# Context products in plain fp32 from the unsplit weights, and ten dot products moved to another place of the order

## The chip, the cores and the metric

One Trainium2 chip, one core of it. The metric is the device time of one execution in microseconds (us), the median of several runs. An execution runs five engines side by side, each with a queue of its own that it works through in order: TensorE (PE, its weight loads PEld), VectorE (DVE), ScalarE (ACT), GpSimd (POOL, idle here) and SyncE (SP), which issues all transfers.

## What is computed

A diffusion backbone of two layers over 1024 latent tokens and 256 context tokens of width 1024. Layer 0 mixes by a gated linear recurrence in both directions, layer 1 by a short convolution, and each is followed by a gated feed-forward part. Shift, scale and gate of each sub-layer come from a product of the conditioning vector with a large matrix. What the change touches is this part of layer 0:

```python
hl = modulate(rms_norm(x, norm_mix_g[l]), sm, cm)
hc = modulate(rms_norm(h_ctx, norm_mix_g[l]), smc, cmc)
ul = seq_conv(hl @ w_x, conv_w, conv_b, CONV_A_PAD)
uc = seq_conv(hc @ w_x, conv_w, conv_b, CONV_A_PAD)
hl_f, hc_f = rglru_direction(ul, uc, w_r[0], b_r[0], w_i[0], b_i[0], lam[0], False)
hl_b, hc_b = rglru_direction(ul, uc, w_r[1], b_r[1], w_i[1], b_i[1], lam[1], True)
yl = (jax.nn.gelu(hl @ w_gate) * (hl_f + hl_b).astype(hl.dtype)) @ w_out
```

The context only gives the recurrence its starting state. `adaln` is `jax.nn.silu(cvec) @ w + b`, split into six vectors.

## The kernel before

Data lies with channels on the 128 partitions, so a vector of width 1024 is eight chunks. To keep fp32 accuracy at the full rate of TensorE, each operand is split into two fp32r halves: the high half is a copy that ScalarE makes (`wh`, `bh`, `uh`), the low half the rest, which VectorE makes by a subtraction (`wl`, `bl`, `ul`). `mm` (L432 and after) issues three matmuls for one product: high by high, high by low, low by high.

The program is written as a list of units, each a function with the weights that it needs as keys. `run_units` (L369) walks the list. Before each unit it issues as many loads as it finds a free raw tile for, and prepares as many weights ahead as it finds free slots for. There are three raw tiles (`raw0`, shown as raw_95, raw_96 and raw_97 in the rows of the order) of 128x1024 in this part of the kernel, and room for three split weights. A raw tile counts as free as soon as the preparation of its weight is written down, since the split empties it.

The calls aren't issued at once: `Plan.record` (L66, its emission L165, which is why all instructions have that one line) collects them, and `Plan.flush` (L121) puts them in order by its own costs and due times, at `open_mx`, at `open_ffn` and at the end. TensorE's instructions keep the order of the units.

`ORDER` (L45) lists the units of layer 0's mixer. `g2` to `g7` are the gate products. `ctx` normalises the context (`ctx_apply`) into hch and hcl, and makes eight units `wx_ctx` (L744), one per chunk m, called xc0 to xc7 here: eight steps of three matmuls of 256 columns, then a convolution by one pass on ScalarE and three on VectorE (`conv_a`). `mx` closes the context's pool (`cs6`, the normalised context, `xc`, `ccb`), flushes, and opens in the same memory the tile `mx`, seven slots of 128x1280, in which the recurrence works. `x4` to `x7` are the latent products with `w_x`, each with a convolution. `us0` splits chunks 0 and 1 of the latent and context u into uh and ul (`u_split`, L727) for the recurrence blocks `r0` and `r1`, and so on in pairs. A block `r0` to `r7` (`ri`, L778) makes the products with two weights (called ri0 and ri1 for r0 and r1), writes them through tanh into slots of mx on ScalarE, and runs the elementwise chain and the two scans on VectorE with exp and sqrt on ScalarE between.

`e6` and `d3`, `d2`, `d1` are the modulation dots (`ahead_dots`, L864): each loads 512 KB of the matrix and reduces it with the conditioning vector in one pass on VectorE. `e` puts the data into slots of mx in turn, `d` into the one tile `acct`. Six stand in `e6`, thirteen in the `d` between the blocks.

Of the kernel before, what the change touches and what calls it, by code (L numbers as in the profile page):

```python
# [8 lines left out]
F32 = mybir.dt.float32  # L9
F32R = mybir.dt.float32r  # L10
AF = mybir.ActivationFunctionType
ALU = mybir.AluOpType

P = 128
D = 1024
KD = 8
SEQ = 1024
HALF = 512
CTX = 256
# [11 lines left out]
for _n, _w in _VEC:  # L31
# [10 lines left out]
DOTS = (0, 0, 0, 1, 1, 2, 2, 2)  # L42


ORDER = ("g2 shift g3 norm g4 g5 ctx mx us0 e6 x4 r0 d3 x5 d2 r1 d2 us2 x6 d1 r2 d1 x7 d1 r3 d1 us4 d1 r4 d1 g6 r5 "  # L45
         "us6 g7 r6 r7")

TABLE = {AF.Silu: (AF.Silu, AF.Tanh), AF.Gelu_apprx_tanh: (AF.Gelu_apprx_tanh, AF.Tanh), AF.Sqrt: (AF.Sqrt,),
         AF.Exp: (AF.Exp, AF.Tanh), AF.Tanh: (AF.Exp, AF.Tanh)}
# [134 lines left out]
def hybrid_kernel(ctx: ExitStack, tc: tile.TileContext, out, xs, cs, c, cc, ada, vecs,  # L184
                  ident, w0, wx, wg, wo, wri, wbi, wbo, wup, wdn):
    nc = Plan(tc)
    V, S, T, G = nc.vector, nc.scalar, nc.tensor, nc.gpsimd
# [20 lines left out]
    def bank():  # L208
        return ptile[:, ring("bank", 4)]
# [6 lines left out]
    def stt(o, a, s, b, op0=ALU.mult, op1=ALU.add, eng=None):  # L216
        (eng or V).scalar_tensor_tensor(out=o, in0=a, scalar=s, in1=b, op0=op0, op1=op1)
# [10 lines left out]
    def act(o, i, f, bias=0.0, scale=1.0):  # L228
        S.activation(o, i, f, bias=bias, scale=scale)
# [21 lines left out]
    def vcol(name, i):  # L251
        return vec[:, VOFF[name] + i:VOFF[name] + i + 1]

    x = xp.tile([P, KD, SEQ], F32, tag="x", name="x")
# [25 lines left out]
    wslots = [(wh0, wl0, i) for i in range(6)]  # L280

    def unit(fn, *keys):
        units.append((fn, keys))
        return len(units) - 1

    class Raw:

        def __init__(self, src, after=-1, pool="raw"):
            self.src, self.after, self.pool, self.left, self.tile = src, after, pool, 0, None

    class Item:

        def __init__(self, key, raws, n, prep, after=-1):
            self.key, self.raws, self.n, self.prep, self.after = key, raws, n, prep, after
            for r in raws:
                r.left += 1

    items = {}

    def wsrc(key):  # L300
        kind = key[0]
        if kind in ("x", "xc"):
            return wx[key[1]]
        if kind == "g":
            return wg[key[1]]
        if kind == "o":
            return wo[key[1]]
        if kind == "ri":
            return wri[key[1]]
        if kind == "bo":  # L310
            return wbo[key[1]]
        return wdn[key[1], key[2], :, 2 * D:]

    def dot(dst, raw, bt, eng=None):

        if eng is G:
            mul(raw, raw, bt, G)
            S.activation(raw, raw, AF.Identity, bias=0.0, scale=1.0, accum_out=dst)
        else:
            V.scalar_tensor_tensor(out=raw, in0=raw, scalar=1.0, in1=bt, op0=ALU.mult, op1=ALU.mult, accum_out=dst)  # L320
# [4 lines left out]
    def weight_item(key):  # L325
        src = wsrc(key)
        n = src.shape[-1]

        def prep(sl, raws):
            hi, lo = flat(sl[0][0], sl[0][2], len(sl))[:, :n], flat(sl[0][1], sl[0][2], len(sl))[:, :n]  # L330
            split(hi, lo, raws[0].tile[:, :n], weight_hi[0])
            return hi, lo
        return Item(key, [Raw(src)], -(-n // HALF), prep)
# [35 lines left out]
    def run_units(nside):  # L369


        stream, seen, last = [], {}, {}
        for i, (_, keys) in enumerate(units):
            for k in keys:
                if k not in seen:
                    seen[k] = i
                    stream.append(items[k] if k in items else weight_item(k))
                    for _ in range(nside(k)):
                        if side:
                            src, dst, bt, eng = side.pop(0)  # L380
                            stream.append(Item(None, [Raw(src)], 0, lambda sl, raws, dst=dst, bt=bt, eng=eng:
                                               dot(dst, raws[0].tile, bt, eng)))
                last[k] = i
        loads = {"raw": [], "s": []}
        for it in stream:
            for r in it.raws:
                if r not in loads[r.pool]:
                    loads[r.pool].append(r)
        free, pos = [True] * 64, 0
        occ, rp = {n: {} for n in loads}, dict.fromkeys(loads, 0)  # L390
        live, np_ = {}, 0
        for i, (fn, keys) in enumerate(units):
            while True:
                moved = False
                for name, todo in loads.items():
                    tiles = raw0 + more.get("raw", []) if name == "raw" else more.get("stage", [])
                    while todo and todo[0].after < i:
                        at = [(rp[name] + j) % len(tiles) for j in range(len(tiles))]
                        at = [j for j in at if j not in occ[name] or not occ[name][j].left]
                        if not at:  # L400
                            break
                        r = todo.pop(0)
                        r.tile = tiles[at[0]]
                        if len(r.src.shape) == 3:
                            nc.sync.dma_start(r.tile.rearrange("p (a b) -> p a b", a=r.src.shape[1]), r.src)
                        else:
                            nc.sync.dma_start(r.tile[:, :r.src.shape[-1]], r.src)
                        occ[name][at[0]] = r
                        rp[name], moved = at[0] + 1, True
                while np_ < len(stream):  # L410
                    it = stream[np_]
                    if it.after >= i or any(r.tile is None for r in it.raws):
                        break
                    n = len(wslots)
                    at = [(pos + j) % n for j in range(n)]
                    at = [j for j in at if j % max(it.n, 1) == 0 and all(free[j:j + it.n])]
                    if not at:
                        break
                    sl = list(range(at[0], at[0] + it.n))
                    if it.n:  # L420
                        pos = (at[0] + it.n) % n
                    for j in sl:
                        free[j] = False
                    for r in it.raws:
                        r.left -= 1
                    live[it.key] = (it.prep([wslots[j] for j in sl], it.raws), sl)
                    np_, moved = np_ + 1, True
                if not moved:
                    break
            fn(*[live[k][0] for k in keys if k[0] != "act"])  # L430
            for k in keys:
                if last[k] == i:  # L432
                    for j in live.pop(k)[1]:
                        free[j] = True

    def mm(ps, w, wi, rh, rl, start, stop, **o):

# [5 lines left out]
    def mmk(ps, w, rhi, rlo, s):  # L443
        n = len(rhi)
        for k in range(n):
            mm(ps[:, s], w, slice(k * P, (k + 1) * P), rhi[k][:, s], rlo[k][:, s], k == 0, k == n - 1)
# [100 lines left out]
    cpx = ExitStack()  # L547
    cp = cpx.enter_context(tc.tile_pool(name="cp", bufs=1))
    cs6 = cp.tile([P, 6, CTX], F32, tag="cs6", name="cs6")
    hch = cp.tile([P, KD, CTX], F32R, tag="hch", name="hch")  # L550
    hcl = cp.tile([P, KD, CTX], F32R, tag="hcl", name="hcl")
    xc = cp.tile([P, KD, CTX], F32, tag="xc", name="xc")
    ccb = cp.tile([P, D], F32, tag="ccb", name="ccb")
    uc = up.tile([P, KD, CTX], F32, tag="uc", name="uc")
# [154 lines left out]
    def ctx_apply():  # L709
        make_ab(1, modc, 0, 0, 1, "norm_mix_g")  # L710
        A, B = ab(1)
        for k in range(KD):
            u = cs6[:, 2 + k % 4]
            stt(u, xc[:, k], A[k], rc[0], ALU.mult, ALU.mult)
            act(hch[:, k], u, AF.Identity, bias=B[k])
            stt(hcl[:, k], u, B[k], hch[:, k].bitcast(F32), ALU.add, ALU.subtract)

    def conv_a(z, u, m):

        n = z.shape[-1]  # L720
        w = [vcol("a_conv_w", t * 8 + m) for t in range(4)]
        act(u, z, AF.Identity, bias=vcol("a_conv_b", m), scale=w[2])
        stt(u[:, 1:], z[:, :n - 1], w[1], u[:, 1:])
        stt(u[:, 2:], z[:, :n - 2], w[0], u[:, 2:])
        stt(u[:, :n - 1], z[:, 1:], w[3], u[:, :n - 1])
# [16 lines left out]
        unit(f, ("x", m))  # L742

    def wx_ctx(m):  # L744
        def f(w):
            z = bank()
            mmk(z, w, [hch[:, k] for k in range(KD)], [hcl[:, k] for k in range(KD)], slice(0, CTX))
            conv_a(z[:, :CTX], uc[:, m], m)
        unit(f, ("xc", m))

    def gate(m):
# [119 lines left out]
    shifts = start()  # L871
    for o in ORDER.split():
        if o[0] == "g":
# [510 lines left out]
    def nside(key):  # L1384
        return 4 if key in (("g", 2), ("g", 3)) else 0
# [59 lines left out]
```

## Time and profile before

| | us |
|---|---|
| median of 3 runs | 2079.51 (2079.14 to 2079.75) |
| the profiled execution | 2082.59 |
| its span | 2080.8 |
| TensorE busy | 2036.8 (98%) |
| VectorE busy | 1764.5 (85%) |
| ScalarE busy | 1049.3 (50%) |

All rows come from the one profiled execution, whose span is the time from its first instruction to its last. Starts are counted from the span's start. A group of equal instructions has its count, its busy time and the mean of one; instructions of one engine overlap at their ends, so that starts lie closer together than the durations tell. What stands behind an arrow is what an engine waited for.

### The profile page before, as it was taken

To read this page: it belongs to the slowest core of one execution; us is meant where nothing else is said; L and a number is where in the kernel's file an instruction comes from. 1 tells how busy PE (TensorE), PEld (TensorE's weight loads), DVE (VectorE), ACT (ScalarE), POOL (GpSimd) and SP (SyncE) were. 2 spreads that over 40 slices of the span, in tenths; PEclk is the share of its full clock that TensorE was granted. 3 is DMA by queue.
4 is the path that set the end of the run, shared out by engine and by line. 5 is a ranking of instruction groups with operands and counts; after the bars stand their busy time and mean duration, and the time that the engine had idled before them with its cause. 6 is when DMAs were issued, how large, how long until landed. Compare 5 with 4: busy or idle time off the path is not lost.

```text
span 2080.8 us, 25029 instructions
## 1 busy us (share of the span) xinstructions
PE 2036.8 (98%) x9218; PEld 1681.5 (81%) x9218; DVE 1764.5 (85%) x2624; ACT 1049.3 (50%) x1574; POOL 0.2 (0%) x4
## 2 busy tenths in 40 slices
PE   8899989999999999999999999999999999999998
PEld 6688877787888888878888788888888888878888
DVE  7998999979888888798769988858988887688867
ACT  6366878546544444535255433435644444464345
POOL 0000000000000000000000000000000000000000
PEclk9999999999999999999999999999999999999999
DMA  7544222551334455565361345652243443474345
GB/s 298 185 169 162 71 81 84 193 167 48 126 132 157 156 174 173 174 199 162 95 194 66 114 164 197 231 192 75 83 136 128 142 137 108 137 236 142 111 140 164
DMA packets 103418, 307.05 MB, mean 148 GB/s; under 512 B 10368, under 2 KB 14720, under 8 KB 103168
## 3 DMA queue, kind: packets, MB, share of 16 engines
q1 hardware_dynamic: 103296, 305.46, 44.6%
q8 instruction: 72, 1.18, 0.2%
q14 instruction: 50, 0.41, 0.1%
HBM read 248.80 MB, written 56.62 MB: 147 GB/s over the span
## 4 chain that ended last, share of the span: by engine, by line
PE 84%; DVE 9%; ACT 4%; DMA 2%; issue 1%; SPq 0%; DVEq 0%; ACTq 0%
PE banks L165 84%; ACT mx L165 2%; DVE x L165 2%; DVE mx L165 2%; DVE u L165 2%; DVE bl L165 2%; DMA x<-in_xs 1%; DVE wl L165 1%; DMA s<-bd 1%; ACT L165 1%; ACT bh L165 1%; DMA raw<-in_wg 0%; DVE uc L165 0%; DVE ul L165 0%; DVE acct L165 0%
## 5 line engine op out<-in xcount | busy, mean ns | idle before, releaser
L165 PE MATMUL banks<-bl,wh 128*128 128x512 f32 (+1 forms) x2720 | 1052.2, 387 | 11.0 <-DVE bl L165 10.9
L165 PE MATMUL banks<-bh,wh 128*128 128x512 f32 (+1 forms) x2720 | 1054.3, 388 | 3.2 <-ACT wh L165 1.6
L165 PE MATMUL banks<-bh,wl 128*128 128x512 f32 (+1 forms) x2720 | 1051.0, 386 | 2.6 <-DVE wl L165 2.5
L165 PEld LDWEIGHTS banks<-bl,wh 128*128 128x128 f32 x2720 | 511.6, 188 | 124.7 <-DVE bl L165 21.6
L165 PEld LDWEIGHTS banks<-bh,wh 128*128 128x128 f32 x2720 | 511.8, 188 | 109.0 <-ACT wh L165 2.0
L165 PEld LDWEIGHTS banks<-bh,wl 128*128 128x128 f32 x2720 | 511.6, 188 | 108.1 <-DVE wl L165 7.3
L165 ACT ACTIVATE wh<-raw 128x512 fp32r<-128x512 f32 (+2 forms) x386 | 275.6, 717 | 475.0 <-PE banks L165 394.7
L165 DVE TENSOR_TENSOR wl<-raw,wh 128x512 fp32r<-128x512 f32 (+2 forms) x386 | 303.2, 794 | 60.4 <-ACT wh L165 56.9
L165 DVE SCALAR_TENSOR_TENSOR x<-banks,mod,x 128x512 f32<-128x512 f32 (+1 forms) x184 | 132.6, 726 | 93.3 <-PE banks L165 92.3
L165 ACT ACTIVATE s<-banks 128x512 f32<-128x512 f32 x174 | 103.8, 596 | 195.0 <-PE banks L165 191.8
L165 ACT ACTIVATE wh<-s 128x512 fp32r<-128x512 f32 x216 | 135.5, 628 | 110.4 <-DVE s L165 63.7
L165 DVE TENSOR_TENSOR wl<-s,wh 128x512 fp32r<-128x512 f32 x216 | 148.5, 688 | 38.6 <-ACT wh L165 34.9
L165 DVE TENSOR_TENSOR s<-s,banks 128x512 f32<-128x512 f32 x158 | 107.8, 683 | 37.4 <-PE banks L165 36.9
L165 DVE SCALAR_TENSOR_TENSOR x<-s,vec,x 128x504 f32<-128x504 f32 x132 | 96.4, 740 | 10.2 <-ACT x L165 9.0
L165 DVE SCALAR_TENSOR_TENSOR acct<-acct,cb 128x1024 f32<-128x1024 f32 x69 | 84.1, 1218 | 4.5 <-DMA acct<-in_ada 4.5
L165 PE MATMUL banks<-uh,wh 128*128 128x512 f32 (+1 forms) x192 | 70.8, 369 | 8.1 <-ACT mx L165 7.0
L165 PE MATMUL banks<-ul,wh 128*128 128x512 f32 (+1 forms) x192 | 70.5, 367 | 3.1 <-DVE ul L165 3.1
L165 PE MATMUL banks<-uh,wl 128*128 128x512 f32 (+1 forms) x192 | 70.2, 366 | 0.0
L165 ACT ACTIVATE bh<-s 128x512 fp32r<-128x512 f32 x88 | 51.5, 624 | 35.3 <-DMA s<-bd 34.0
L165 ACT ACTIVATE bh<-x,cols 128x512 fp32r<-128x512 f32 x64 | 45.1, 721 | 42.1 <-DVE cols L165 27.3
L165 DVE TENSOR_TENSOR x<-x,s 128x512 f32<-128x512 f32 x90 | 61.0, 686 | 0.8
L165 DVE TENSOR_TENSOR bl<-s,bh 128x512 fp32r<-128x512 f32 x88 | 57.2, 684 | 5.0 <-ACT bh L165 5.0
(154 smaller groups left out, 1702.0 us busy)
## 6 DMA issues: line engine op xcount, KB each, us to landing
raw<-in_wup SPq DMA_DIRECT2D x92, 512.0 KB, 3.6
acct<-in_ada SPq DMA_DIRECT2D x69, 512.0 KB, 3.5
bd<-x SPq DMA_DIRECT2D x48, 512.0 KB, 3.2
s<-bd SPq DMA_DIRECT2D x44, 512.0 KB, 4.5
raw<-in_wdn SPq DMA_DIRECT2D x32, 512.0 KB, 4.4
raw<-in_wdn SPq DMA_DIRECT2D x40, 384.0 KB, 3.4
raw<-in_wbi SPq DMA_DIRECT2D x26, 512.0 KB, 4.1
u<-in_ada SPq DMA_DIRECT2D x24, 512.0 KB, 4.6
```

Source lines behind the costliest of these rows:

```text
L165: getattr(getattr(self.tc.nc, e), op)(*a, **k)
```

## The change

The products of the context no longer use split operands. `wx_ctx` takes the raw weight tile as it was loaded and the normalised context in one fp32 tile `hc`, and issues one plain fp32 matmul for each of the eight steps. Its item is marked `hold`: the raw tile stays taken until the unit is done. The two context tiles hch and hcl become the one `hc`. In the order, `e6` becomes `e16`, and of the thirteen dots in `d` ten go: three `d1` are left.

```diff
-ORDER = ("g2 shift g3 norm g4 g5 ctx mx us0 e6 x4 r0 d3 x5 d2 r1 d2 us2 x6 d1 r2 d1 x7 d1 r3 d1 us4 d1 r4 d1 g6 r5 "
-         "us6 g7 r6 r7")
+ORDER = "g2 shift g3 norm g4 g5 ctx mx us0 e16 x4 r0 x5 r1 us2 x6 d1 r2 x7 d1 r3 us4 d1 r4 g6 r5 us6 g7 r6 r7"
...
-        def __init__(self, key, raws, n, prep, after=-1):
-            self.key, self.raws, self.n, self.prep, self.after = key, raws, n, prep, after
+
+        def __init__(self, key, raws, n, prep, after=-1, hold=False):
+            self.key, self.raws, self.n, self.prep, self.after, self.hold = key, raws, n, prep, after, hold
             for r in raws:
                 r.left += 1
...
-        if kind in ("x", "xc"):
+        if kind == "x":
             return wx[key[1]]
...
                     for r in it.raws:
-                        r.left -= 1
-                    live[it.key] = (it.prep([wslots[j] for j in sl], it.raws), sl)
+                        r.left -= not it.hold
+                    live[it.key] = (it.prep([wslots[j] for j in sl], it.raws), sl, it.raws if it.hold else [])
                     np_, moved = np_ + 1, True
...
                 if last[k] == i:
-                    for j in live.pop(k)[1]:
+                    _, sl, held = live.pop(k)
+                    for j in sl:
                         free[j] = True
+                    for r in held:
+                        r.left -= 1
...
-    hch = cp.tile([P, KD, CTX], F32R, tag="hch", name="hch")
-    hcl = cp.tile([P, KD, CTX], F32R, tag="hcl", name="hcl")
+    hc = cp.tile([P, KD, CTX], F32, tag="hc", name="hc")
...
             stt(u, xc[:, k], A[k], rc[0], ALU.mult, ALU.mult)
-            act(hch[:, k], u, AF.Identity, bias=B[k])
-            stt(hcl[:, k], u, B[k], hch[:, k].bitcast(F32), ALU.add, ALU.subtract)
+            act(hc[:, k], u, AF.Identity, bias=B[k])
...
     def wx_ctx(m):
+
         def f(w):
             z = bank()
-            mmk(z, w, [hch[:, k] for k in range(KD)], [hcl[:, k] for k in range(KD)], slice(0, CTX))
+            for k in range(KD):
+                T.matmul(z[:, :CTX], w[:, k * P:(k + 1) * P], hc[:, k], start=k == 0, stop=k == KD - 1)
             conv_a(z[:, :CTX], uc[:, m], m)
+        items["xc", m] = Item(("xc", m), [Raw(wx[m])], 0, lambda sl, rs: rs[0].tile, hold=True)
         unit(f, ("xc", m))
```

What this does to the order of the queues stands at three places. First SP's queue from the loads of the last context weights on (in_wx are the weights of xc and x, in_wri those of the blocks, in_ada the rows of the dots). Before:

```order
L165 DMA raw_96<-in_wx 128x1024
L165 DMA raw_97<-in_wx 128x1024
L165 DMA raw_95<-in_wri 128x1024
L165 DMA raw_96<-in_wri 128x1024
L165 DMA raw_97<-in_wx 128x1024
L165 DMA raw_95<-in_wx 128x1024
L165 DMA raw_96<-in_wri 128x1024
L165 DMA mx_1235<-in_ada 128x1024 x6
L165 DMA acct_73<-in_ada 128x1024
```

With the change, from the loads of xc7 (raw_96) and x4 (raw_97) on:

```order
L164 DMA raw_96<-in_wx 128x1024
L164 DMA raw_97<-in_wx 128x1024
L164 DMA raw_95<-in_wx 128x1024
L164 DMA raw_97<-in_wri 128x1024
L164 DMA raw_96<-in_wri 128x1024
L164 DMA raw_97<-in_wri 128x1024
L164 DMA raw_97<-in_wx 128x1024
L164 DMA mx_1082<-in_ada 128x1024 x16
L164 DMA raw_97<-in_wri 128x1024
```

Before, x4, ri0, ri1 and x5 take the three tiles in turn (raw_97, raw_95, raw_96, raw_97). Now all four go into raw_97, each behind the split of the one before it, because raw_95 and raw_96 are held for xc6 and xc7; what frees these two goes to x6 (raw_95) and the first weight of r2 (raw_96). The loads of the dots stand behind them, sixteen in one row instead of six.

VectorE's queue around block r0. Before, from the low half of ri1's split on:

```order
L165 TENSOR_TENSOR wl_94<-raw_96,wh_93 128x1024
L165 SCALAR_TENSOR_TENSOR uc_109<-banks_72,vec_75,uc_109 128x255
L165 SCALAR_TENSOR_TENSOR uc_109<-banks_72,vec_75,uc_109 128x254
L165 SCALAR_TENSOR_TENSOR uc_109<-banks_72,vec_75,uc_109 128x255
L165 TENSOR_TENSOR ul_112<-u_110,uh_111 128x1024 x2
L165 TENSOR_TENSOR ul_112<-uc_109,uh_111 128x256 x2
L165 SCALAR_TENSOR_TENSOR mx_1235,mod_78<-mx_1235,cb_74 128x1024 x2
L165 SCALAR_TENSOR_TENSOR x_85<-banks_72,vec_75,x_85 128x1023
L165 SCALAR_TENSOR_TENSOR x_85<-banks_72,vec_75,x_85 128x1022
L165 SCALAR_TENSOR_TENSOR x_85<-banks_72,vec_75,x_85 128x1023
L165 TENSOR_TENSOR wl_94<-raw_97,wh_93 128x1024
L165 SCALAR_TENSOR_TENSOR mx_1235,mod_78<-mx_1235,cb_74 128x1024 x4
```

With the change, from the splits of ri0 and ri1 on:

```order
L164 TENSOR_TENSOR wl_94<-raw_97,wh_93 128x1024 x2
L164 TENSOR_TENSOR ul_111<-u_109,uh_110 128x1024 x2
L164 SCALAR_TENSOR_TENSOR x_85<-banks_72,vec_75,x_85 128x1023
L164 SCALAR_TENSOR_TENSOR x_85<-banks_72,vec_75,x_85 128x1022
L164 TENSOR_TENSOR ul_111<-uc_108,uh_110 128x256 x2
L164 SCALAR_TENSOR_TENSOR mx_1082,mod_78<-mx_1082,cb_74 128x1024 x2
L164 SCALAR_TENSOR_TENSOR x_85<-banks_72,vec_75,x_85 128x1023
L164 TENSOR_TENSOR wl_94<-raw_97,wh_93 128x1024
L164 SCALAR_TENSOR_TENSOR mx_1082,mod_78<-mx_1082,cb_74 128x1024 x10
L164 SCALAR_TENSOR_TENSOR mx_1082<-mx_1082,u_109 128x1024
L164 SCALAR_TENSOR_TENSOR mx_1082,mod_78<-mx_1082,cb_74 128x1024 x3
L164 SCALAR_TENSOR_TENSOR u_109<-mx_1082,u_109 128x1024
```

The rows with mod_78 are dots, x_85 the convolution of x4, ul the low halves of u for r0 and r1. The splits of ri0 and ri1 now follow each other, ahead of ul; twelve dots instead of six stand ahead of the first elementwise step of r0 (mx<-mx,u), three more ahead of the second.

ScalarE's queue at the same place. Before, from the high half of ri1's split (raw_96) on:

```order
L165 ACTIVATE wh_93<-raw_96 128x1024
L165 ACTIVATE uc_109<-banks_72,vec_75 128x256
L165 ACTIVATE uh_111<-u_110 128x1024 x2
L165 ACTIVATE uh_111<-uc_109 128x256 x2
L165 ACTIVATE x_85<-banks_72,vec_75 128x1024
L165 ACTIVATE wh_93<-raw_97 128x1024
```

With the change, from the split of x4 on:

```order
L164 ACTIVATE wh_93<-raw_97 128x1024
L164 ACTIVATE uc_108<-banks_72,vec_75 128x256
L164 ACTIVATE wh_93<-raw_97 128x1024 x2
L164 ACTIVATE uh_110<-u_109 128x1024 x2
L164 ACTIVATE x_85<-banks_72,vec_75 128x1024
L164 ACTIVATE uh_110<-uc_108 128x256 x2
L164 ACTIVATE wh_93<-raw_97 128x1024
```

The uh copies still stand behind the split of ri1, which now is the third of the splits out of raw_97.

## Rows read from the trace of the kernel before

**Rows 1.** Engine totals: busy us, share of the span, instructions.

```profile
PE 2036.8 (98%) x9218; PEld 1681.5 (81%) x9218; DVE 1764.5 (85%) x2624; ACT 1049.3 (50%) x1574; POOL 0.2 (0%) x4
```

**Rows 2.** Busy time by stage: stretch, length, PE, PEld, DVE, ACT, POOL, clock, DMA, GB/s.

```profile
146.80:169.80 23.00, 23.00 (x193) 23.00 (x192) 20.61 (x32) 12.58 (x16) 0.00 (x0) 1.00 0.49 160
...
205.60:393.30 187.70, 174.75 (x814) 145.11 (x813) 184.05 (x184) 149.87 (x158) 0.00 (x0) 0.96 0.26 86
```

**Rows 3.** Waits of TensorE, 170 to 420 us: total us, times, longest.

```profile
PE banks L165 <- ACT mx L165: 7.0, 2, 4.3
...
PEld banks L165 <- ACT mx L165: 9.0, 4, 4.8
```

**Rows 4.** Timeline (start, us): the first context product, and the matmul behind the last.

```profile
146.79 0.28 PE L165 MATMUL banks<-hch,wh 128*128 128x256 f32 x1
...
169.83 0.40 PE L165 MATMUL banks<-bh,wh 128*128 128x512 f32 x1
```

**Rows 5.** Timeline around a plain fp32 matmul of 256 columns (cs,ones, two records).

```profile
124.36 0.40 PE L165 MATMUL banks<-bh,wl 128*128 128x512 f32 x1
124.36 0.42 PEld L165 LDWEIGHTS banks<-cs,ones 128*128 128x128 f32 x2
124.59 0.59 PE L165 MATMUL banks<-cs,ones 128*128 128x256 f32 x2
...
125.25 0.40 PE L165 MATMUL banks<-bl,wh 128*128 128x512 f32 x1
125.48 0.39 PE L165 MATMUL banks<-bh,wl 128*128 128x512 f32 x1
```

**Rows 6.** Groups, 0 to 420 us: the halves of a weight's split (busy, mean ns).

```profile
L165 DVE TENSOR_TENSOR wl<-raw,wh 128x1024 fp32r<-128x1024 f32 x39 | 47.2, 1218 | 3.2 <-ACT wh L165 3.1
...
L165 ACT ACTIVATE wh<-raw 128x1024 fp32r<-128x1024 f32 x39 | 40.7, 1055 | 32.1 <-PE banks L165 22.6 <-issue 6.2 <-DMA raw<-in_wg 2.0
```

**Rows 7.** Transfers issued from 130 to 240 us, with the median us to landing.

```profile
raw<-in_wx SPq DMA_DIRECT2D x10, 512.0 KB, 4.3
raw<-in_wri SPq DMA_DIRECT2D x6, 512.0 KB, 4.0
mx<-in_ada SPq DMA_DIRECT2D x6, 512.0 KB, 7.2
```

**Rows 8.** Transfers issued from 187 to 230 us, when few others ran.

```profile
raw<-in_wri SPq DMA_DIRECT2D x3, 512.0 KB, 3.4
```

**Rows 9.** Timeline before and at block r0, ScalarE, SP, VectorE, TensorE.

```profile
171.32 2.00 ACT L165 ACTIVATE uh<-u 128x1024 fp32r<-128x1024 f32 x2
...
172.63 3.17 SPq L165 DMA_DIRECT2D mx<-in_ada  x6
...
173.57 2.35 DVE L165 TENSOR_TENSOR ul<-u,uh 128x1024 fp32r<-128x1024 f32 x2
175.84 0.75 DVE L165 TENSOR_TENSOR ul<-uc,uh 128x256 fp32r<-128x256 f32 x2
177.86 1.22 DVE L165 SCALAR_TENSOR_TENSOR mx<-mx,cb 128x1024 f32<-128x1024 f32 x1 [1.27 <-DMA mx<-in_ada]
...
180.74 0.39 PE L165 MATMUL banks<-uh,wh 128*128 128x512 f32 x1
...
187.14 1.22 DVE L165 SCALAR_TENSOR_TENSOR mx<-mx,cb 128x1024 f32<-128x1024 f32 x1
...
188.29 1.22 DVE L165 SCALAR_TENSOR_TENSOR mx<-mx,cb 128x1024 f32<-128x1024 f32 x1
```

**Rows 10.** Groups of VectorE, 169.8 to 393.3 us: the thirteen dots in acct.

```profile
L165 DVE SCALAR_TENSOR_TENSOR acct<-acct,cb 128x1024 f32<-128x1024 f32 x13 | 15.8, 1217 | 0.0
```

**Rows 11.** Busy time from the end of ul on, to and behind the end of r0.

```profile
176.60:223.10 46.50, 45.99 (x225) 38.85 (x225) 38.48 (x41) 32.35 (x34) 0.00 (x0) 1.00 0.31 112
223.10:393.30 170.20, 157.76 (x729) 130.74 (x728) 166.72 (x171) 136.33 (x143) 0.00 (x0) 0.96 0.27 88
```

**Rows 12.** Busy time of one stretch, with the granted clock behind POOL.

```profile
270.00:300.00 30.00, 23.94 (x96) 19.35 (x97) 29.64 (x33) 22.28 (x25) 0.00 (x0) 0.83 0.28 88
```

## The prediction

> **What bounds the kernel now.** I read the engine totals first, then the windows by stage, the waits of TensorE, the order of the queues, and last the timeline around the change. Over the whole span TensorE is busy 98%, VectorE 85% [rows 1], so later stages pass any delay on. The change touches one stretch, in which the bound changes hands [rows 2]. The context products, 146.8 to 169.8 us, keep TensorE busy throughout, VectorE for 20.6 of 23.0 us. From 205.6 to 393.3 us, the recurrence blocks, VectorE is busy 184.05 of 187.7 us and TensorE has 13 us idle; what TensorE waits for there are tanh writes of ScalarE into the mx slots, 7.0 and 9.0 us [rows 3], and these wait for VectorE to free a slot. So a microsecond of VectorE's work is worth most after 205 us, and one of TensorE's inside the context products. The change takes dots from the first place and pays in the second. What decides is when the dots and the weights of the first block can start.
>
> **The change, part by part.**
>
> The products. Before, 192 matmuls of 256 columns run from 146.79 to 169.83 us [rows 4]: 23.04 us, 0.120 each. After there are 64 plain fp32 ones. Their price stands in one place: the fp32 matmul of 256 columns at 124.59, two records, lies between bh,wl at 124.36 and bl,wh at 125.25; those 0.89 us hold it and two ordinary matmuls of 0.227 (125.25 to 125.48), so it costs 0.89 - 0.454 = 0.436 us, with its two weight loads [rows 5]. 64 x 0.436 = 27.9 us: **TensorE +4.9 us**, 3.49 us a product instead of 2.88, ending at 174.7 instead of 169.8. Starts are read to 0.01 us, so it is at least 0.425; if each record took as long as an ordinary 512-column matmul it would be 0.454: +4.2 to +6.0.
>
> Weight loads, against a rule. The fp32 pair's two weight loads take 0.42 us together and lie beside the matmul [rows 5]. The Trainium skill (TensorE: Matmul & The Clock Gate, section Weight-path perf modes) says that the fast weight load is off for FP32 operands, which speaks against this change. By its 128 columns at 1.2 GHz, an estimate of 0.107 us, 128 loads that nothing hid would add 13.7 us. The row shows them hidden, and my sum has nothing for them; the other case is a rival below.
>
> Splits that fall away. Eight context weights are no longer split: 8 x 1.055 us on ScalarE and 8 x 1.22 on VectorE [rows 6] (a little less there, since neighbours overlap at their ends), and eight hcl halves. That is some 12 us of VectorE's time, but it lies before 171 us, where TensorE is the bound; it buys nothing unless something useful takes its place. By the order nothing does: the sixteen dots load into mx, which lies on the context pool's memory, and their loads stand in SP's queue behind the raw loads of x4, ri0, ri1 and x5.
>
> The held tiles. This is the main term. A context weight now keeps its raw tile until its products are done, so xc6 and xc7 hold raw_95 and raw_96, and x4, ri0, ri1 and x5 all pass through raw_97, one load and one split after the other. Loads take 4.3, 4.0 and, alone, 3.4 us from issue to landing [rows 7, 8]. xc5 ends at 146.8 + 6 x 3.49 = 167.7 and frees raw_97 at 167.9. x4: landed 172.2, ScalarE's half 173.3, VectorE's (behind the conv of xc6) 174.6, just in time for TensorE at 174.7. ri0: landed 178.6, split 180.9. ri1: landed 184.3, ScalarE 185.4, VectorE 186.6. ScalarE's uh copies for block r0, 1.0 us each [rows 9], stand behind ri1's split in its queue, VectorE's ul behind its other half: ul 0 and 1 end at 187.7 and 188.8. Before, they ended at 175.9, 5 us ahead of block r0 at 180.7 [rows 9]. After, TensorE is through x4 at 185.6 and reaches the product that needs ul 1 at 186.5: it stalls 2.3 us. VectorE then does two of x4's three conv passes (2.5 us) and the two small ul halves: 192.0. Before it stood there, without those passes, at 176.6 [rows 9]: **VectorE is 15.4 - 2.5 = 12.9 us late.** x5's load goes out at 186.6 and the dots' behind it; the first mx load landed 5.2 us after its issue before (172.6 to 177.8 [rows 7, 9]), so the first dot runs at about 192.2.
>
> A price by a rule. The Trainium skill (DMA: Bandwidth & Descriptors, section Anatomy of one DMA) fits 2.0 us plus the bytes at 436 GB/s, 3.2 us for 512 KB, measured on another issue path; by that estimate the three loads would take 9.6 us, not 11.7, and the time would be 2.1 us lower. No load here landed in under 3.4 us [rows 7, 8], so I keep the rows.
>
> The dots. Nineteen dots follow that point on VectorE in either version, 6 + 13 before [rows 10] and 16 + 3 after, 1.145 us apart where they follow each other (starts at 187.14 and 188.29 [rows 9]). So the ten buy no time after it; moving them only changes what VectorE's idle time hides. Twelve of them now stand ahead of the first elementwise step of r0 instead of six, and they reuse the seven mx slots into which r0's tanh values must go, so ScalarE's tanh waits for dots that wait for loads. At the end of r0 I make VectorE 192.0 + 38.5 (its work from 176.6 to 223.1 [rows 11]) + 9 x 1.145 more dots - 2.5 = 238.3 us without any idle time, against 223.1.
>
> Idle time, the only thing to win back. From 176.6 to 393.3 us VectorE idled 8.0 + 3.5 = 11.5 us before [rows 11], most of it inside r0. After: about 3 us up to the end of r0 (dots waiting for the second round of slots, and the exp to sqrt chain), the same 3.5 later, and 2 us because nine dots that covered waits for ScalarE are gone there (10.3 us of work; I take a fifth as uncovered, bounds none and all). Sum 8.5.
>
> **Sum:** 12.9 - 11.5 + 8.5 = +9.9 us at the end of block r7. TensorE doesn't set that end: it has 170.2 - 157.8 = 12.4 us idle after 223 [rows 11]. Behind it everything is as before with a few splits exchanged, 0 with no cover in it: TensorE is nearly full, and the delay passes on. The profiled execution is 2082.59 us (span 2080.8 and 1.8 around it), so its counterpart would be 2092.5; it lies 3.1 above the median of the runs, 2079.51, and on that I predict **2089.4 us**. With no idle time left it would be 12.9 - 11.5 = +1.4; with all ten us uncovered +18; loads of 3.4 or 4.5 us shift it by 2 either way.
>
> **Rivals.**
> VectorE catches up: the order after r0, freed of dots, closes nearly all gaps. For: 3.5 us idle in 170 were all that was left before, so it is a packed queue; against: it must be packed in r0 too, where loads and slots pace it. +1.4 to +4 us, 2081 to 2083.5.
> The relief wins (the other side): the recurrence is VectorE's, ten dots fewer there are 11.5 us, less the products' 4.9, so -6.6 and 2072.9. It decides if the sixteen dots are done by the end of x4, about 186 us, in VectorE's idle time. For: the 98% busy blocks; against: SP's order, in which their loads come after x5's, by my chain at 187.
> Weight loads of plain fp32 don't hide behind the matmuls: 64 pairs of 0.42 us [rows 5] are 26.9 us more on TensorE, 2116 with the rest. Against: the one pair in the trace hid them.
> A second delay: TensorE's stalls at r0 and r1 let its clock fall, as after the idle stretch from 270 us, when TensorE was busy 23.94 of 30 us and the mean granted clock was 0.83 of full speed, a third of the time at the lower level of 1.2 GHz [rows 12]. That lost 30 x 0.17 = 5.1 us there; on top of the forecast 2094.5.
> That the change doesn't do what its words say is in the forecast: the dots come after the products, not beside them.
>
> **How the numbers follow.** A measurement of this kernel can tell about 0.2% (4.2 us) from no change. Forecast 0.62, with +4.5 to +16; second delay 0.12; unhidden loads 0.04: slower 0.78. VectorE catches up 0.15: same. Relief wins 0.07: faster. The range leaves out the relief, the unhidden loads and part of the catching up: 2081.0 to 2097.0.
>
> **What would show it.** Right: 64 fp32 products at 0.43 to 0.45 us, 27 to 29 us together; in the waits, TensorE or ScalarE waiting for uh, ul or wh at about 185 to 189 us; the four loads into raw_97 one behind the other's split; the first mx load issued near 187; VectorE largely idle from 147 to 190, and r0 ended near 240 us; r7's end near 403. Wrong: mx loads issued before 180, r0 ended before 232, products over 0.5 us each, or VectorE with well over 10 us idle after 240.

## The result, and the profile after

The changed kernel took **2092.12 us** (median of 6 runs, 2091.31 to 2093.06), the kernel before beside it 2079.63 (2079.04 to 2081.68): a ratio of 1.0059, 95% interval 1.0046 to 1.0072, **12.5 us slower**. The profiled execution took 2093.05 us, its span 2091.3.

The group of the context products, TensorE from 140 to 180 us (busy us, mean ns), is the counterpart of the 192 matmuls of [rows 4]:

```profile
L164 PE MATMUL banks<-hc,raw 128*128 128x256 f32 x128 | 27.8, 379 | 0.0
```

128 records are 64 matmuls: 0.434 us each, 27.8 us in place of 23.2. Busy time by stage, cut at the start of these products, 2.7 us behind their end, at the end of the split of u, at the end of r0 and of r7 (columns as in [rows 2]):

```profile
144.20:174.80 30.60, 30.60 (x142) 26.76 (x142) 12.71 (x25) 6.48 (x10) 0.00 (x0) 1.00 0.42 139
174.80:189.20 14.40, 12.69 (x47) 9.54 (x46) 7.84 (x9) 6.78 (x8) 0.00 (x0) 0.89 0.49 177
189.20:238.20 49.00, 44.34 (x209) 36.79 (x208) 46.28 (x58) 31.12 (x33) 0.00 (x0) 0.96 0.53 194
238.20:402.10 163.90, 152.68 (x717) 126.16 (x715) 157.11 (x154) 134.29 (x141) 0.00 (x0) 0.98 0.20 63
```

VectorE, nearly full beside the context products before [rows 2], is busy 12.71 of 30.6 us, then 7.84 of 14.4: the dots don't lie beside the products. ScalarE's timeline shows what it waits for:

```profile
169.08 1.04 ACT L164 ACTIVATE wh<-raw 128x1024 fp32r<-128x1024 f32 x1
...
175.78 1.06 ACT L164 ACTIVATE wh<-raw 128x1024 fp32r<-128x1024 f32 x1 [3.15 <-DMA raw<-in_wri]
181.46 1.06 ACT L164 ACTIVATE wh<-raw 128x1024 fp32r<-128x1024 f32 x1 [4.61 <-DMA raw<-in_wri]
182.42 1.99 ACT L164 ACTIVATE uh<-u 128x1024 fp32r<-128x1024 f32 x2
...
195.43 1.48 ACT L164 ACTIVATE mx<-banks,vec 128x1024 f32<-128x1024 f32 x2 [6.65 <-DVE mx L164]
...
206.29 1.12 ACT L164 ACTIVATE mx<-banks,vec 128x1024 f32<-128x1024 f32 x1 [4.36 <-DVE mx L164]
210.08 1.12 ACT L164 ACTIVATE mx<-banks,vec 128x1024 f32<-128x1024 f32 x1 [2.67 <-DVE mx L164]
```

The first three are the splits of x4, ri0 and ri1, whose loads go one after the other into the one raw tile; the copies uh stand behind them. Then r0's tanh waits for VectorE, whose dots occupy the mx slots. VectorE, for [rows 9], and its last step of r7:

```profile
183.69 2.35 DVE L164 TENSOR_TENSOR ul<-u,uh 128x1024 fp32r<-128x1024 f32 x2
...
188.47 0.75 DVE L164 TENSOR_TENSOR ul<-uc,uh 128x256 fp32r<-128x256 f32 x2
189.14 1.22 DVE L164 SCALAR_TENSOR_TENSOR mx<-mx,cb 128x1024 f32<-128x1024 f32 x1
...
400.86 1.23 DVE L164 TENSOR_TENSOR x<-u,mx 128x1024 f32<-128x1024 f32 x1
```

r7 ends at 402.1, 8.7 us later than the 393.4 before. But the context products started 2.5 us earlier here, at 144.25 against 146.79, and a second profile of the kernel before (below) shows that 2.1 us of this come without the change. So all places are counted from the start of these products. The ends come from the timelines: the last small ul half, and VectorE's last step `x<-x,mx` of r0 and `x<-u,mx` of r7. Ratios are against the kernel before on the same chip.

| kernel | products start | ul done | r0 done | r7 done | median us | ratio (95%) |
|---|---|---|---|---|---|---|
| before | 146.79 | 29.80 | 74.10 | 246.60 | 2079.63 | 1 |
| before, again | 144.69 | 29.80 | 74.11 | 246.48 | 2080.08 | one run |
| changed | 144.25 | 44.97 | 93.97 | 257.84 | 2092.12 | 1.0059 (1.0046 to 1.0072) |
| e1 products only | 145.12 | 45.11 | 87.00 | 256.93 | 2090.78 | 1.0048 (1.0032 to 1.0065) |
| e2 dots only | 146.91 | 29.81 | 83.71 | 247.53 | 2082.27 | 1.0007 (0.9998 to 1.0016) |
| e3 own tiles | 145.02 | 36.33 | 90.61 | 254.55 | 2089.04 | 1.0041 (1.0026 to 1.0056) |
| e4 own tiles, old order | 144.01 | 36.40 | 82.80 | 252.04 | 2086.52 | 1.0026 (1.0016 to 1.0036) |
| e9 no chain | 144.36 | 32.88 | 87.53 | 250.67 | 2085.44 | 1.0025 (1.0014 to 1.0036) |
| e10 no chain, old order | 144.32 | 32.88 | 78.69 | 249.38 | 2083.07 | 1.0019 (1.0009 to 1.0028) |
| e5 ten dots beside | 144.22 | 32.88 | 78.68 | 245.65 | 2079.78 | 0.9997 (0.9987 to 1.0006) |
| e6 thirteen beside | 144.29 | 34.02 | 78.68 | 246.19 | 2079.99 | 0.9998 (0.9989 to 1.0007) |
| e7 split, four beside | 145.68 | 32.54 | 74.10 | 243.68 | 2077.46 | 0.9988 (0.9978 to 0.9997) |
| e11 split, five beside | 144.46 | 33.24 | 78.21 | 243.56 | 2076.73 | 0.9985 (0.9976 to 0.9994) |

The two profiles of the kernel before agree within 0.12 us at r7, so differences of a few tenths can be read in these columns, as far as two profiles of one kernel can tell.

### The profile page after: what moved, and what is told of

Its sections match the earlier page's. It is cut to its first block, busy times and chain, and to the rows that moved or that the text cites. A ratio compares the mean times of both kernels' runs of the same rounds, so it can differ in the third digit from the quotient of the medians.

```text
span 2091.3 us, 24853 instructions
## 1 busy us (share of the span) xinstructions
PE 2039.5 (98%) x9154; PEld 1679.4 (80%) x9154; DVE 1753.0 (84%) x2608; ACT 1040.9 (50%) x1566; POOL 0.2 (0%) x4
## 4 chain that ended last, share of the span: by engine, by line
PE 81%; DVE 12%; ACT 3%; DMA 2%; issue 2%; SPq 0%; DVEq 0%; ACTq 0%
PE banks L164 81%; DVE mx L164 3%; DVE u L164 2%; DVE bl L164 2%; DVE x L164 2%; ACT mx L164 2%; DVE wl L164 1%; DVE ul L164 1%; DMA s<-bd 1%; DMA mx<-in_ada 0%; ACT L164 0%; ACT bh L164 0%; DVE acct L164 0%; DMA x<-in_xs 0%; DMA raw<-in_wri 0%
## 5 line engine op out<-in xcount | busy, mean ns | idle before, releaser
L164 ACT ACTIVATE wh<-raw 128x512 fp32r<-128x512 f32 (+2 forms) x378 | 267.2, 710 | 469.7 <-PE banks L164 384.2
L164 DVE TENSOR_TENSOR wl<-raw,wh 128x512 fp32r<-128x512 f32 (+2 forms) x378 | 293.6, 786 | 67.7 <-ACT wh L164 64.3
L164 DVE SCALAR_TENSOR_TENSOR acct<-acct,cb 128x1024 f32<-128x1024 f32 x59 | 71.9, 1219 | 2.0 <-DMA acct<-in_ada 2.0
L164 DVE TENSOR_TENSOR x<-x 128x512 f32<-128x512 f32 x88 | 60.1, 686 | 0.7
```

The costliest lines, as they stand in the source:

```text
L164: getattr(getattr(self.tc.nc, e), op)(*a, **k)
```

## The experiments

### Undoing one half of the change: e1 and e2

The changed kernel with the old `ORDER`, and the kernel before with the new one:

```diff
-ORDER = "g2 shift g3 norm g4 g5 ctx mx us0 e16 x4 r0 x5 r1 us2 x6 d1 r2 x7 d1 r3 us4 d1 r4 g6 r5 us6 g7 r6 r7"
+ORDER = ("g2 shift g3 norm g4 g5 ctx mx us0 e6 x4 r0 d3 x5 d2 r1 d2 us2 x6 d1 r2 d1 x7 d1 r3 d1 us4 d1 r4 d1 g6 r5 "
+         "us6 g7 r6 r7")
```

> The change's fp32 products and held tiles, with the order of before (six dots ahead of block r0, thirteen between the blocks). Theory A (the held tiles make VectorE about 12.7 us late at block r0, and the dots' place matters little): the four loads still go through raw_97 one after the other, the small ul halves of r0 end near 189 us as in the changed kernel, and the time is 2088 to 2092 us. Theory B (the sixteen dots ahead of block r0, which occupy the slots that its tanh values need, are the cost): without them 2082 to 2085 us. Theory C (only the 4.6 us that the products cost TensorE are passed on): 2084 to 2085 us, and the same for the other runs with fp32 products.

> The kernel before with nothing but the new order of the dots (e16, three d1); products stay split, no tile is held. Theory A: the weights of r0 and r1 arrive as before, the small ul halves end near 176.6 us, and the time stays within 3 us of 2079.6 (nineteen dots follow that point in either order). Theory B: the dots ahead of r0 hold its tanh values up, 2086 us or more. Theory C: 2079.6, nothing.

e1: 2090.78, +10.7 us on the kernel before beside it (2080.03). e2: 2082.27, +2.2, with no change just inside the interval. Theories B and C fall, as e1 lies above their ranges: nearly all of the loss comes with the products and their held tiles, 1.7 to 2.2 with the dots. But e2 shows that the dots ahead of r0 do hold up its tanh. ScalarE's timeline of e2:

```profile
187.45 2.99 ACT L164 ACTIVATE mx<-banks,vec 128x1024 f32<-128x1024 f32 x4 [4.24 <-DVE mx L164]
...
198.65 1.12 ACT L164 ACTIVATE mx<-banks,vec 128x1024 f32<-128x1024 f32 x1 [2.98 <-DVE mx L164]
202.50 1.12 ACT L164 ACTIVATE mx<-banks,vec 128x1024 f32<-128x1024 f32 x1 [2.73 <-DVE mx L164]
```

r0 ends 9.6 us later than before, and the blocks behind it, freed of ten dots, give 8.7 back (247.53 - 83.71 = 163.8 us instead of 172.5). That is why moving the dots costs so little at the end.

### Taking the serial loads away: e3 and e4, then e9 and e10

xc6 and xc7 get tiles of their own, the halves of `xc`, free once the context is normalised; e3 has the new order of dots, e4 the old one:

```diff
+    more["c"] = [xc[:, i:i + 4].rearrange("p k c -> p (k c)") for i in (0, 4)]
...
-        items["xc", m] = Item(("xc", m), [Raw(wx[m])], 0, lambda sl, rs: rs[0].tile, hold=True)
+        items["xc", m] = Item(("xc", m), [Raw(wx[m], len(units) - 6 if m > 5 else -1, "c" if m > 5 else "raw")], 0, lambda sl, rs: rs[0].tile, hold=True)
```

> The changed kernel, but the weights xc6 and xc7 load into the two halves of the tile xc, which is free once the context is normalised, so that x4, ri0 and ri1 get a raw tile each. Theory A: the serial chain is gone, ul of r0 is done before 180 us, TensorE does not wait for it, VectorE's lateness of 12.7 us shrinks to about 1; with 16 dots to fill its waits the time is 2076 to 2083 us. Theory B: the dots stay ahead of r0, so 2088 us or more. Theory C: 2084 to 2085 us.

> As the run before it (tiles of their own for xc6 and xc7), with the order of dots of the kernel before: fp32 products without the chain and without the moved dots. Theory A: within 3 us of the run before it, 2077 to 2084 us, since TensorE has 12 us idle in the recurrence to take up its 4.6. Theory B: 2079 to 2085 us, clearly under the run before it. Theory C: 2084 to 2085 us.

2089.04 and 2086.52: faster than the changed kernel, yet both above what theory A gave; e3 lies where theory B put it, e4 above all three ranges. They were no clean test. In their order of SP's queue x4, ri0, ri1 and x5 still pass through one tile, now raw_95, only earlier, and ScalarE still waits for ri1's load in e3:

```profile
176.09 1.06 ACT L164 ACTIVATE wh<-raw 128x1024 fp32r<-128x1024 f32 x1 [2.67 <-DMA raw<-in_wri]
```

The reason is that `run_units` writes loads down ahead. When xc3's tile comes free, xc4 and xc5 hold the others, so the next three loads all take this one. e9 and e10 make x4, ri0 and ri1 wait in the list until another tile is free for each:

```diff
-        return Item(key, [Raw(src)], -(-n // HALF), prep)
+        return Item(key, [Raw(src, start_at.get(key, -1))], -(-n // HALF), prep)
...
+        if 2 < m < 6:
+            start_at[(("x", 4), ("ri", 0), ("ri", 1))[m - 3]] = len(units)
```

> The two runs with tiles of their own were no clean test: x4, ri0 and ri1 still went one after the other through the raw tile that xc3 had left, ri1's split ending at 177 to 178 us. Here x4, ri0 and ri1 may only load once xc3, xc4 and xc5 are through, so that each takes another tile; xc6 and xc7 as before in the halves of xc; the order of the dots is the changed kernel's. Theory A', counted from the start of the context products: 4.6 us of the products pass in full to the end of block r0 (through TensorE and tanh, as in the run with ten dots beside), the chain is worth the rest of the change's 11.3 us at the end of r7 but for the 1.0 of the moved dots: about 5.7 us. So without the chain the small ul halves end about 33 us after the start of the context products, r7 at 252 instead of 257.8, and the time is 2085 to 2088 us. Rival F (the chain hides behind the products anyway): as the run with tiles of their own, 2089 us or more.

> As the run before it, with the order of dots of the kernel before, so that only the products themselves are left of the change. Theory A': the end of r0 is 4.6 us later than in the kernel before, counted from the start of the context products (78.7 instead of 74.1), r7's at 251 instead of 246.6, and the time is 2084 to 2086 us. Rival G (the 4.6 us are taken up by idle time of TensorE in the recurrence, as the prediction said): 2079 to 2082 us.

Now ScalarE of e10 makes the last split right behind the conv of xc6, waiting for no load, and uh follows the conv of xc7:

```profile
169.16 1.04 ACT L165 ACTIVATE wh<-raw 128x1024 fp32r<-128x1024 f32 x1
172.15 0.56 ACT L165 ACTIVATE uc<-banks,vec 128x256 f32<-128x256 f32 x1 [1.94 <-PE banks L165]
172.61 2.00 ACT L165 ACTIVATE uh<-u 128x1024 fp32r<-128x1024 f32 x2
```

Measured: 2085.44 (+6.0) and 2083.07 (+3.6). Rival F falls: against the changed kernel and e1 the chain is worth 12.5 - 6.0 = 6.5 and 10.7 - 3.6 = 7.2 us by the medians (the intervals of the ratios leave 3.5 to 4 us to either side), at the end of r7 7.2 and 7.5. Theory A' gave 5.7, so by these it put the chain too low and the products too high. e10's median lies between the ranges of A' and G, and its interval, +1.9 to +5.8 us, reaches into both; its trace decides: the end of r0 is 4.6 us late as A' had it, that of r7 2.8, where A' had 4.4 and G almost nothing. The busy time of e10 by stage (the products, to r0's end, to r7's end), and the two later stages of the kernel before:

```profile
144.30:172.10 27.80, 27.80 (x130) 24.47 (x129) 13.52 (x24) 7.81 (x11) 0.00 (x0) 1.00 0.46 151
172.10:223.00 50.90, 50.39 (x246) 42.46 (x245) 42.12 (x49) 33.25 (x37) 0.00 (x0) 1.00 0.38 135
223.00:393.70 170.70, 158.08 (x739) 131.03 (x737) 167.73 (x171) 138.31 (x146) 0.00 (x0) 0.97 0.26 85
```

```profile
170.00:220.90 50.90, 50.39 (x245) 42.45 (x245) 42.54 (x49) 34.08 (x38) 0.00 (x0) 1.00 0.38 135
220.90:393.40 172.50, 160.06 (x739) 132.58 (x737) 169.02 (x173) 138.53 (x146) 0.00 (x0) 0.96 0.27 87
```

From the products' end to the end of r0 both take 50.90 us with TensorE busy 50.39 of them, while VectorE idles over 8 us in each. ScalarE's first tanh of r0, in the kernel before and in e10, waits for TensorE's bank, not for a slot:

```profile
183.66 1.12 ACT L165 ACTIVATE mx<-banks,vec 128x1024 f32<-128x1024 f32 x1 [0.57 <-PE banks L165]
```

```profile
185.76 1.12 ACT L165 ACTIVATE mx<-banks,vec 128x1024 f32<-128x1024 f32 x1 [0.56 <-PE banks L165]
```

That is 36.87 and 41.44 us after the start of the products. So that stretch is TensorE's, and the 4.6 us pass through it whole (e7 below is the check on this). Only behind r0 are 1.8 us of them won back.

### The dots truly beside the products: e5, e6, e7, e11

e5 puts ten dots beside the fp32 products, e6 thirteen, on the tiles of e3. e7 and e11 keep the split products of the kernel before, with four and five beside; e11 also has seven in `e`:

```diff
+    def beside():
+        b = [x[:, 7], x[:, 6], acct.rearrange("p a b -> p (a b)"), cs6[:, :4].rearrange("p k c -> p (k c)"), ccb]
+        return b[ring("beside", len(b))]
...
             for m in range(KD):
                 wx_ctx(m)
+                call(ahead_dots, [mods.pop(0) for _ in range(10 * (m + 1) // KD - 10 * m // KD)], beside)
```

> The words of the change done in earnest: fp32 products, xc6 and xc7 in tiles of their own, six dots in e, and the other ten beside the context products, in tiles that are free there (two chunks of x, acct, and cs6 and ccb once the context is normalised). Theory A, as the runs so far leave it: the 4.6 us of the products pass on to block r0 because VectorE's split of u stands behind the convolutions of the context; of the 11.5 us of work that ten dots take from between the blocks some 8.6 are won (in the runs with sixteen dots ahead of r0 the stretch from the end of r0 to the end of r7 is 8.5 us shorter). 6.5 - 8.6 = -2.1: 2076 to 2080 us, and VectorE busy over 20 us of the 31 of the context products. Rival D (no room on the transfers: ten more loads of 512 KB delay the context weights and TensorE waits for them): 2083 to 2090 us, with TensorE idle between 145 and 180 us.

> As the run before it with all thirteen of the dots between the blocks beside the context products. Theory A: another 2 to 3 us less, 2074 to 2078 us. Rival D: the same as the run before it or worse, over 2080 us, TensorE idle in the context products waiting for weights.

> The kernel before with its split products, and four of the thirteen dots between the blocks moved beside the context products, where VectorE has 2.4 us idle and 5 more up to the first dot of e6. Theory A: four dots are 4.6 us of VectorE's work, three quarters of it won if they fit: 2076 to 2078 us, and without any fp32 product; if VectorE is too full there, the split of u comes later and the time stays at 2079 to 2081 us. Rival E (VectorE's work between the blocks is not what sets the end of r7): 2079.6 us, no change.

> The version without fp32 products that was faster than before, one step further: five dots beside the split context products, seven in e (the seventh slot of mx, no slot used twice), seven between the blocks. If VectorE's idle time ahead of block r0 (5.3 us from the split of u to the end of r0 in the run with four) takes them, another 1 to 2 us less: 2075 to 2077 us. If they come on top of a path that is paced by TensorE and tanh: 2077.5 us or more.

e5 by stage, cut as e10 above:

```profile
144.22:172.01 27.79, 27.79 (x130) 24.48 (x129) 21.36 (x38) 7.80 (x11) 0.00 (x0) 1.00 0.66 231
172.01:222.90 50.89, 50.39 (x245) 42.47 (x245) 41.96 (x49) 33.23 (x37) 0.00 (x0) 1.00 0.37 135
222.90:389.90 167.00, 156.34 (x733) 130.39 (x732) 157.36 (x150) 138.47 (x147) 0.00 (x0) 0.97 0.17 56
```

The dots fit: VectorE 21.36 of 27.79 us, TensorE without a gap, so rival D falls. But the time is that of the kernel before (2079.78 against 2079.79): just inside theory A's range, though not by its sum, which had 8.6 us won by the ten dots. Against e10 ten dots fewer take 10.4 us off VectorE's work behind r0 (167.73 to 157.36) and only 3.7 off the length (170.70 to 167.00); VectorE's idle time there grows from 3 to 9.6 us. Three dots more, e6, bring nothing that shows: the expected 2 to 3 us fail to appear. So the relief of ten dots is worth a third of the work moved, and the fp32 products that make room for it cost as much.

Without fp32 products the same idea does gain a little. e7: 2077.46, 2.3 us under the kernel before, its interval just clear of no change, and its two stages behind the products are no longer than before. From the products' end to the end of r0:

```profile
168.87:219.80 50.93, 50.42 (x246) 42.48 (x245) 45.42 (x56) 34.11 (x38) 0.00 (x0) 1.00 0.36 135
```

Here ul ends 2.7 us late (32.54 against 29.80), nearly as late as in e10, and yet r0 ends on time (74.10): a split of u that is 3 us late costs r0 nothing where TensorE isn't late, so what e10 carries to the end of r0 is the time of the products on TensorE. Behind r0 four dots fewer are worth 2.9 of their 4.6 us, where ten in e5 were worth 3.7 of 10.4. e11 by stage:

```profile
144.46:167.65 23.19, 23.19 (x194) 23.19 (x193) 22.30 (x35) 12.67 (x17) 0.00 (x0) 1.00 0.57 182
167.65:222.70 55.05, 55.05 (x267) 46.48 (x266) 49.80 (x62) 37.56 (x41) 0.00 (x0) 1.00 0.37 134
222.70:388.00 165.30, 153.52 (x718) 126.89 (x716) 159.95 (x158) 134.33 (x141) 0.00 (x0) 0.97 0.22 72
```

**e11 is the fastest of all, 2076.73 us, 2.8 under the kernel before** (0.9985, 0.9976 to 0.9994) and 15 under the changed one. It is not told apart from e7: r7 ends at 243.56 and 243.68. The dot that it has more in `e` holds the end of r0 up by 4.1 us (78.21), so VectorE's idle time ahead of r0 did not take it, as its expectation had it; the stage behind is shorter by as much.

### The kernel before once more: e8

> The kernel before, unchanged, a second profile: where do its context products start? If the 146.8 us of the first profile was a run's luck with TensorE's clock (it ran at the lower level from 110.9 to 116 us after an idle gap), another profile may show 144 to 145 us, as the changed kernel's does, and its span is then about 2 us shorter. If the split of the context's operands delays them, it shows 146.8 again.

From 110 to 117 us, the first profile of the kernel before, then the second:

```profile
110.00:117.00 7.00, 7.00 (x21) 5.81 (x22) 6.19 (x13) 6.17 (x12) 0.00 (x0) 0.55 0.54 177
```

```profile
110.00:117.00 7.00, 7.00 (x25) 5.60 (x25) 6.19 (x13) 6.35 (x11) 0.00 (x0) 0.76 0.54 189
...
144.69 0.28 PE L165 MATMUL banks<-hch,wh 128*128 128x256 f32 x1
```

The same program, a granted clock of 0.55 and of 0.76: a run's luck. The products start 2.1 us earlier, and the span is 2078.3 instead of 2080.8. Not all of the 2.1 us is this clock: the matmul behind the idle gap that precedes the slow stretch starts 0.7 us earlier already, so 1.4 us are left for it. The first profile, then the second:

```profile
109.91 1.41 PE L165 MATMUL banks<-ones,cs 128*128 128x1 f32 x6 [2.44 <-DVE u L165]
```

```profile
109.22 0.80 PE L165 MATMUL banks<-ones,cs 128*128 128x1 f32 x6 [2.44 <-DVE u L165]
```

## Why the prediction was right, and where its steps were not

The forecast was 2089.4 us, 9.9 us slower, within 2081.0 to 2097.0; measured are 2092.12 and 12.5 us slower, the largest part of it by the chain of loads that it named as its main term.

**The products.** 64 at 0.434 us, 27.8 us, against 0.436 and 27.9. The weight loads hid, as the row of the one fp32 matmul had said: TensorE is busy throughout.

**The splits that fall away** bought nothing: VectorE idles 17.9 of the 30.6 us of the changed kernel's first stage.

**The held tiles.** The chain came as worked out. The splits of ri0 and ri1 begin 31.5 and 37.2 us after the start of the products; the predicted landings, 178.6 and 184.3, were 31.8 and 37.5 after it. The last small ul half ends 15.2 us late, less the 2.5 of conv work done already 12.7, predicted 12.9. That the chain is the main term stands: 6.5 to 7.2 us of the 12.5, by e9 and e10.

**What failed here** is the step that made the chain the whole of VectorE's lateness, with TensorE's +4.9 us hidden inside it because "TensorE doesn't set that end". Without any chain ul is still 3.1 us late (32.88 against 29.80), since the split of u stands behind the convolution of the last context product on both engines, and r0 still ends 4.6 us late, through TensorE and not through ul, as e7 shows. Behind r0, where the prediction pointed to 12.4 us of idle TensorE, 1.8 of these are won back and not all. The sum was not hurt, as the lateness of ul held both.

**The dots.** r0 was to end near 241 us (238.3 and 3 of idle time), 94.2 after the start of the products; it ended at 93.97. That moving them gains nothing and costs little is right, but not free: +1.7 (the changed kernel against e1), +2.2 (e2), +2.4 us (e9 against e10).

**The idle time** was the mis-sized term: 8.5 us predicted from the end of ul to that of r7, 9.5 measured. Up to the end of r0 it was 2.7 against 3 (49.00 - 46.28); behind it 6.8 against 5.5 (163.90 - 157.11). Of the waits for ScalarE that nine dots had covered more came to light than the fifth that was assumed: idle time there was 3.5 before, so 3.3 us are new where the prediction had 2.

**The sum.** r7 ends 257.84 - 246.60 = 11.2 us late, predicted 9.9. Of the difference 1.0 us is that idle time; the rest is VectorE's work behind r0, 157.11 us where the prediction's rows leave 166.72 - 10.3 = 156.4. The other 1.3 us of the 12.5 lie behind r7, where the prediction had 0. From r7's end to the end of the span the profiles show 1689.2 us for the changed kernel, 1687.4 and 1687.1 for that before, and 1686.5 to 1689.0 in the experiments with the same stages behind r7, so this may be scatter between runs; no run settles it.

In all: products about 3.6 us, chain about 7, moved dots about 2, by the medians, each known to a few us only.

**The rivals.** That VectorE catches up: it did not, r7 is 11 us late. Unhidden weight loads: no. A second delay by TensorE's clock: the clock did fall to 0.89 at r0, but what r0's tanh waited for then was VectorE's dots (6.65, 4.36 and 2.67 us in the rows above). The relief: it was to decide if the dots were done early, and by SP's order they could not be; its price, -6.6 us, was too high as well, since e5, where they are done early, gains nothing over the kernel before. Setting the profiled execution 3.1 us above the median was right: e8 shows 2.1 us of that in the start of the products, which is a run's scatter.

## What to carry to other kernels

A product that reads its operand straight from the load buffer holds that buffer until the product is done; before making the change, follow the next loads through the buffers that remain, in the order in which the list assigns them, because one free buffer makes a chain of load, split, load. Work that covers waits on its engine is worth less than its duration when it is moved away: ten dots of 1.15 us bought 3.7 us, four of them 2.9. Where two engines take turns as the bound, ask which of them paces the stretch right behind the edit: the 4.6 us on TensorE were passed on whole up to the end of r0.

## What was not expected of the hardware

After the same idle gap of 2.44 us the same program was granted a clock of 0.55 of full speed in one run and 0.76 in another over the same 7 us, and with it the context products moved by 1.4 us of the 2.1 between the two profiles. Two profiles should be aligned at the start of the changed stage before their ends are compared.
